# Hybrid RWKV-7 layer on one core: the jobs beside the triangular inverse in three pieces, the bonus sums later, the woven products spread to the inverse's middle

## The chip, the cores and the metric

One core of one Trainium2 chip runs the whole layer. The metric is the device time of one execution in microseconds (us), as the median of several runs.

## What is computed

One layer of a backbone that joins a bidirectional RWKV-7 recurrence and a neighbourhood attention, for 128 context tokens and 512 latent tokens of width 1024, all in float32. The change touches the recurrence alone. For every head (8 of them, 64 channels each) and each of two directions it is

```python
def _wkv_step(s, inp):
    r, w, k, v, a, b = inp
    sa = jnp.einsum("bhvk,bhk->bhv", s, a)
    s = s * w[:, :, None, :] + sa[..., None] * b[:, :, None, :] + v[..., None] * k[:, :, None, :]
    return s, jnp.einsum("bhvk,bhk->bhv", s, r)
...
    k_bonus = _heads(0.5 * (k_dir[:, :, 0] + k_dir[:, :, 1]))
    bonus = jnp.sum(rh * k_bonus * r_k, axis=-1, keepdims=True) * vh
    out = (y.astype(u.dtype) + bonus).reshape(bsz, t_len, RW_WIDTH) * gate
```

The kernel doesn't step through the tokens one by one. It cuts them into 10 chunks of 64 and solves each chunk with the inverse of a triangular matrix.

## The kernel before

**Groups and lines.** The 512 channels of the recurrence are four groups, ct = 0 to 3, of 128 channels (two heads). In a group there are 20 lines: 10 chunks in each direction. The groups run one after the other, and each has these stages, written as generators:

- `main`: the products that fill the triangular matrices Nt (`n_job`).
- `inv`: the inverse of all the 32x32 triangular blocks at once, on DVE, in 30 steps s (the multiplications L1315, L1322, L1329 and additions L1333), then two transposes (RT at L1346, T at L1348), products with the inverse on PE (L1359 and L1373), a copy on ACT (Hs, L1364) and copies on DVE and ACT into Rt (L1367, L1378).
- `carry`: the chunks in their order. Its first use of Rt is the matmul at L1449.
- `out`: the output of the group (L1498 to L1509), which runs beside the next group's inverse.

**Jobs.** The inverse is work of DVE. Beside it PE does jobs, at the steps s that the table `jobs` names. In groups 0 to 2 these are steps 2, 9 and 28, in group 3 steps 2, 8 and 28: a job of four lines first, then two jobs of eight lines. A job is `t_job` (L1274: transposes of B and K as 64x64 matmuls, 64 of them for eight lines, copied by ACT into TG) and then `g_job`, which has for each line two matmuls of the values (`turn`, L1252, or `flip`, L1263), two of L1216 (into the buffer pg) and four of L1219 (into the buffers pr): 128 matmuls for eight lines. `g_job` returns a function `masks`, which DVE runs at a later step (table `mds`; L1233 for pg and L1236 for pr). All of pg, pr, the t_job's buffers, and those of the bonus and of `out` are PSUM tiles of one tag, "w", with six buffers (`wps`).

**Bonus.** `bonus` is a generator too: one DVE operation (L1156), then for each half of the columns a matmul with a matrix of ones (L1162) and a DVE operation that multiplies it with v (L1164, in the trace by its tile bv).

**Woven products.** Between all of this PE does big products of other parts of the layer (L223 and L587; 128x128 weights, 320 columns), which depend on nothing of the group. `weave` sets the order: after each `yield` of a stage it takes one element "a.b.c" of the table `plan`, issues a products from the stream `fill`, b steps of the previous group's `out` and c steps of `bonus`.

```python
                p = next(plan)
                for _ in range(p[0]):
                    if not next(fill, False):
                        break
...
                weave(inv(ct, S, late), (og, bg))
```

The stream `fill` also carries the steps that are put off until so many products later. One of them is the shift of the next group's r and k (`shift`: L551 on ACT, L552 and L554 on DVE, tiles rt_ and kt_, first 128 columns, then 512). PE, DVE, ACT and POOL run these stages in the order in which the program is written (`manual_schedule`), so the plan decides what stands behind what on each engine.

Of the kernel before, what the change touches and what calls it, by code (L numbers as in the profile page):

```python
# [17 lines left out]
H2 = 320  # L18
# [13 lines left out]
        ("0.0.0 2.0.0 2.0.1 10.0.0 2.0.1 2.0.1 2.0.1 2.0.1 2.0.1 2.0.0 10.0.0 2.0.0 2.0.0 10.0.0 2.0.0 "  # L32
         "2.0.0 2.0.0 10.0.0 2.0.0 2.0.0 2.0.0 2.0.0 2.0.0 2.0.0 2.0.0 2.0.0 2.0.0 2.0.0 2.0.0 2.0.0 "
         "5.0.0 24.0.0 20.0.0 10.0.0 8.0.0 8.0.0 0.0.0"),
# [3 lines left out]
        ("0.0.0 0.0.0 2.0.1 10.0.0 1.0.0 2.1.1 2.1.1 2.1.1 2.1.1 1.1.1 10.0.0 3.1.0 2.0.0 2.0.0 2.0.0 "  # L38
         "2.1.0 2.1.0 10.0.0 2.1.0 2.1.0 2.1.0 2.1.0 2.1.0 2.1.0 12.0.0 2.0.0 2.0.0 2.0.0 2.0.0 2.0.0 "
         "5.0.0 24.0.0 20.0.0 10.0.0 8.0.0 8.0.0 0.0.0"),  # L40
# [3 lines left out]
        ("0.0.0 10.0.0 2.0.1 10.0.0 2.0.0 2.1.1 2.1.1 2.1.2 2.1.1 2.1.0 10.0.0 2.0.0 2.0.0 2.0.0 2.1.0 "  # L44
         "2.1.0 2.1.0 10.0.0 2.1.0 2.1.0 2.1.0 3.1.0 4.1.0 2.1.0 2.0.0 2.0.0 2.0.0 4.0.0 2.0.0 2.0.0 "
         "5.0.0 24.0.0 18.0.0 8.0.0 9.0.0 8.0.0 0.0.0"),
# [3 lines left out]
        ("0.0.0 16.1.0 8.1.1 9.0.0 2.1.0 8.1.1 1.1.1 0.1.1 0.1.1 0.1.1 4.1.0 14.1.0 6.1.0 6.1.0 6.1.0 "  # L50
         "6.1.0 6.1.0 7.1.0 6.0.0 6.0.0 6.0.0 6.0.0 6.0.0 6.0.0 7.0.0 6.0.0 6.0.0 6.0.0 6.0.0 6.0.0 "
         "6.0.0 6.0.0 11.0.0 8.0.0 8.0.0 2.0.0 0.0.0"),
# [25 lines left out]
    h2=0.91, jobs=((2, 9, 28), (2, 9, 28), (2, 9, 28), (2, 8, 28)),  # L78
    mds=((4, 12), (4, 12), (4, 12), (4, 12)), bud=((1.8, 0.8), (1.3, 1.8)), off=6, tk=2, h3=1,
# [35 lines left out]
def body(ctx: ExitStack, tc: tile.TileContext, xs, xp, cols, consts, w_ada, b_row, w_rw, w_qkv,  # L115
# [986 lines left out]
    with ExitStack() as s3:  # L1102
# [52 lines left out]
        def bonus(ct, S):  # L1155
            dve.scalar_tensor_tensor(out=S.bv, in0=S.bv, scalar=dcol(dhrk, ct), in1=rt_,  # L1156
                                     op0=ALU.mult, op1=ALU.mult)
            yield
            for hf in range(2):
                hs_ = slice(hf * H2, (hf + 1) * H2)  # L1160
                ps = wps()
                pe.matmul(ps[:, :H2], kc("blk1", 128), S.bv[:, hs_], start=True, stop=True)  # L1162
                yield
                dve.tensor_tensor(out=S.bv[:, hs_], in0=ps[:, :H2], in1=v[:, hs_], op=ALU.mult)  # L1164
                yield
            marks.add(f"R{ct}")
# [35 lines left out]
        def g_job(S, l0, l1):  # L1202
# [5 lines left out]
            for l in range(l0, l1):  # L1208
                if l0 == 0:
                    turn(pv, l, 0)  # L1210
                if l0 > 8:
                    flip(pv, l, f0)
                o_ = slice(64 * (l - l0), 64 * (l - l0) + 64)
                b, k = (S.BK[l // 10][:, l % 10, i, :] for i in range(2))
                for h in range(2):
                    pe.matmul(pg[hrows[1 - h], o_], k[hrows[h], :], AG[hrows[h], l, h, :], start=True, stop=True)  # L1216
                for x, i in ((b, 0), (k, 1)):
                    for h in range(2):
                        pe.matmul(pr[h][hrows[h ^ i], o_], x[hrows[h], :], R_[hrows[h], l, :],  # L1219
                                  start=True, stop=True)  # L1220
# [18 lines left out]
            return masks  # L1239
# [54 lines left out]
        def inv(ct, S, late):  # L1294
# [10 lines left out]
            masks = []  # L1305
            for s in range(1, 31):
# [870 lines left out]
```

## Time and profile before

| | |
|---|---|
| runs of the kernel, device us | 1145.75, 1146.5, 1142.03; median 1145.75 |
| the profiled execution's own time | 1141.53 us |
| its span in the profile | 1139.8 us, granted clock 0.997 |
| PE busy (matmuls) | 1106.1 us, 97% |
| DVE busy | 781.1 us, 69% |
| ACT busy | 533.7 us, 47% |
| POOL busy | 193.7 us, 17% |
| four groups of the recurrence, about 240 to 600 us of the span | PE busy 345.4 of 360 us |

How to read it: PE is TensorE, DVE VectorE, ACT ScalarE, POOL GpSimd. The span is the profiled execution from its first to its last record; the metric's time of that execution is 1.73 us longer. Busy shares are averages over the span. The rows below come from lists of waits and from timelines, whose times count from the span's start.

### The profile page before, as it was taken

To read this page: it belongs to the slowest core of one execution; us is meant where nothing else is said; L and a number is where in the kernel's file an instruction comes from. 1 tells how busy PE (TensorE), PEld (TensorE's weight loads), DVE (VectorE), ACT (ScalarE), POOL (GpSimd) and SP (SyncE) were. 2 spreads that over 40 slices of the span, in tenths; PEclk is the share of its full clock that TensorE was granted. 3 is DMA by queue.
4 is the path that set the end of the run, shared out by engine and by line. 5 is a ranking of instruction groups with operands and counts; after the bars stand their busy time and mean duration, and the time that the engine had idled before them with its cause. 6 is when DMAs were issued, how large, how long until landed. Compare 5 with 4: busy or idle time off the path is not lost.

```text
span 1139.8 us, 26864 instructions
## 1 busy us (share of the span) xinstructions
PE 1106.1 (97%) x11160; PEld 979.3 (86%) x11160; DVE 781.1 (69%) x1646; ACT 533.7 (47%) x1056; POOL 193.7 (17%) x261
## 2 busy tenths in 40 slices
PE   6999999999999999999899999999999999999998
PEld 4688878799888988888898788999899989998997
DVE  4565465769658948946777846996478647864776
ACT  4444566664574565566353525654134413441340
POOL 1163244320101211111100511200001010101000
PEclk9999999999999999999999999999999999999999
DMA  9752677654423443343734961223112321232122
GB/s 342 266 107 97 191 263 264 200 152 111 126 65 96 115 121 94 107 110 98 276 97 134 260 215 64 90 77 120 65 59 90 114 72 56 93 108 77 56 94 93
DMA packets 60482, 149.16 MB, mean 131 GB/s; under 512 B 7460, under 2 KB 22436, under 8 KB 60360
## 3 DMA queue, kind: packets, MB, share of 16 engines
q1 hardware_dynamic: 54312, 129.85, 35.0%
q0 software_dynamic: 4032, 14.68, 6.6%
q10 hardware_dynamic: 2016, 2.90, 0.8%
q8 instruction: 88, 1.44, 0.5%
q14 instruction: 34, 0.28, 0.1%
HBM read 118.41 MB, written 14.32 MB: 116 GB/s over the span
## 4 chain that ended last, share of the span: by engine, by line
PE 71%; DVE 11%; issue 7%; ACT 5%; DMA 5%; POOL 1%; SPq 0%; ACTq 0%; DVEq 0%; POOLq 0%
PE acc L311 23%; PE f L1880 21%; PE fl L223 9%; PE mm L223 4%; DMA wa<-in_w_ada_dram 2%; DVE RL L1333 1%; DVE pr L1329 1%; PE po L1011 1%; PE psa L1049 1%; PE pt L993 1%; PE lg L964 1%; DMA win<-in_rpbp_dram 1%; PE w L1449 1%; PE fl L587 1%; PE w L1462 1%
## 5 line engine op out<-in xcount | busy, mean ns | idle before, releaser
L1880 PE MATMUL f<-t,whi 128*128 128x320 f32 x640 | 141.7, 309 | 0.2
L311 PE MATMUL acc<-whi,u 128*128 128x512 f32 (+1 forms) x448 | 136.0, 385 | 0.0
L1880 PE MATMUL f<-b,whi 128*128 128x320 f32 x608 | 135.0, 310 | 0.4 <-DVE b L212 0.4
L223 PE MATMUL fl<-h,whi 128*128 128x320 f32 x672 | 121.6, 321 | 0.0
L1880 PEld LDWEIGHTS f<-t,whi 128*128 128x128 f32 x640 | 106.8, 188 | 0.8 <-issue 0.4
L223 PEld LDWEIGHTS fl<-h,whi 128*128 128x128 f32 x672 | 101.5, 188 | 4.9
L192 ACT CAST whi<-wst 128x1024 fp32r<-128x1024 f32 (+1 forms) x77 | 79.3, 1033 | 54.6 <-PE acc L311 28.3
L1880 PEld LDWEIGHTS f<-b,whi 128*128 128x128 f32 x608 | 101.7, 188 | 1.1 <-issue 0.6
L1880 PE MATMUL f<-t,wlo 128*128 128x320 f32 x320 | 98.9, 309 | 0.0
L311 PEld LDWEIGHTS acc<-whi,u 128*128 128x128 f32 x448 | 83.5, 188 | 16.6
L1880 PE MATMUL f<-b,wlo 128*128 128x320 f32 x304 | 94.0, 309 | 0.0
L1933 ACT CAST whi<-ws 128x1024 fp32r<-128x1024 f32 x40 | 42.0, 1051 | 104.5 <-PE f L1880 45.6
L311 PE MATMUL acc<-wlo,u 128*128 128x512 f32 (+1 forms) x224 | 86.3, 385 | 0.0
L1947 POOL TENSOR_TENSOR ws<-wst 128x512 f32<-128x512 f32 x20 | 28.9, 1447 | 334.9 <-DVE wlo L1936 226.3
L195 DVE TENSOR_TENSOR wlo<-wst,whi 128x1024 fp32r<-128x1024 f32 (+2 forms) x57 | 60.2, 1066 | 28.2 <-ACT whi L192 27.7
L311 PE MATMUL acc<-whi,h 128*128 128x512 f32 x240 | 78.5, 401 | 0.7 <-DVE h L436 0.7
L1748 DVE SCALAR_TENSOR_TENSOR tt<-acc,G 128x512 f32<-128x512 f32 (+1 forms) x51 | 34.7, 680 | 59.9 <-PE acc L311 44.6
L223 PE MATMUL fl<-h,wlo 128*128 128x320 f32 x336 | 63.3, 320 | 0.0
L1933 ACT CAST whi<-wst 128x1024 fp32r<-128x1024 f32 (+1 forms) x48 | 41.4, 870 | 42.3 <-PE acc L311 37.6
L191 POOL DMA_DIRECT2D wlo<-wst x28 | 24.8, 886 | 210.8 <-ACT wlo L190 194.9
L1880 PEld LDWEIGHTS f<-t,wlo 128*128 128x128 f32 x320 | 60.1, 188 | 0.0
L1936 DVE TENSOR_TENSOR wlo<-ws,whi 128x1024 fp32r<-128x1024 f32 x40 | 55.4, 1385 | 5.4 <-ACT whi L1933 5.4
(341 smaller groups left out, 2528.5 us busy)
## 6 DMA issues: line engine op xcount, KB each, us to landing
wst<-in_w_dram SPq DMA_DIRECT2D x66, 512.0 KB
wst<-in_w_rw_dram SPq DMA_DIRECT2D x31, 512.0 KB
wlo<-wst POOLq DMA_DIRECT2D x28, 512.0 KB, 4.8
wa<-in_w_ada_dram SPq DMA_DIRECT2D x24, 512.0 KB
f<-in_w_ada_dram SPq DMA_DIRECT2D x16, 512.0 KB
wst<-in_w_qkv_dram SPq DMA_DIRECT2D x12, 512.0 KB
o<-o_d SPq DMA_DIRECT2D x14, 320.0 KB
x<-in_xs_dram SPq DMA_DIRECT2D x8, 512.0 KB
```

The lines of the kernel that those rows point to most:

```text
L191: pool.dma_start(lo[:, :n].bitcast(F32), st[:, :n], accum_op=ALU.add)
L192: act.copy(hi[:, :n], st[:, :n])
L195: dve.tensor_tensor(out=lo[:, a:b], in0=st[:, a:b], in1=hi[:, a:b].bitcast(F32), op=ALU.subtract)
L223: pe.matmul(ps[:, :t1 - t0], w[:, a:a + 128], x[:, k0 + kt, t0:t1], start=n == 0, stop=n == 3 * nk - 1)
L311: pe.matmul(pss[i][:, a:b], lhs(x, kt, ts_), w[:, cs_], start=ki == 0 and n == 0, stop=ki == last and n == 2)
L587: pe.matmul(ps[hf][:, :H2], u[:, kt * 128:kt * 128 + 128], x[:, kt, a:b], start=kt == 0 and n == 0, stop=kt == 7 and n == 2)
L964: pe.matmul(psl[:, hd, o_:o_ + n], qT[ft][rows, qs], x[rows, :], start=True, stop=True)
L1748: dve.scalar_tensor_tensor(out=tt, in0=ps[:, a:b], scalar=c, in1=G[:, g, sl], op0=ALU.mult, op1=ALU.mult)
L1880: pe.matmul(ps[:, :H2], w_[:, c_], x_[:, kt, :], start=first and kt + n == 0, stop=last and kt == 3 and n == 2, skip_group_check=more)
L1933: act.copy(r[0][:, :width], src())
L1936: dve.tensor_tensor(out=r[1][:, :width], in0=src(), in1=r[0][:, :width].bitcast(F32), op=ALU.subtract)
L1947: eng_x(PRM["se"][i - 1]).tensor_tensor(out=o_, in0=x, in1=y, op=op)
```

## The change

1. `g_job` becomes a generator with one `yield` in its middle. For the jobs after step 5, `inv` runs `t_job` at step s, the first four lines of `g_job` at step s + 1 and the last four at step s + 2, so that a plan element, with its products, stands in each of the two gaps. The four-line job at step 2 is run at once as before.
2. The third job starts at step 26, not 28; in group 3 the second at step 9, not 8. The second masks are run at step 14, not 12.
3. In `bonus` both matmuls stand together, and the two DVE operations come later, one plan element apart.
4. The table `plan`: the number of products of each inverse is the same, but elements at the inverse's end give some to its middle. For group 2's inverse:

```diff
-        ("0.0.0 10.0.0 2.0.1 10.0.0 2.0.0 2.1.1 2.1.1 2.1.2 2.1.1 2.1.0 10.0.0 2.0.0 2.0.0 2.0.0 2.1.0 "
-         "2.1.0 2.1.0 10.0.0 2.1.0 2.1.0 2.1.0 3.1.0 4.1.0 2.1.0 2.0.0 2.0.0 2.0.0 4.0.0 2.0.0 2.0.0 "
-         "5.0.0 24.0.0 18.0.0 8.0.0 9.0.0 8.0.0 0.0.0"),
+        ("0.0.0 10.0.0 2.0.1 10.0.0 2.0.1 2.1.0 2.1.0 2.1.1 2.1.1 2.1.0 4.0.0 5.0.0 6.0.0 3.0.0 3.1.0 3.1.0 3.1.0 "
+         "6.0.0 3.1.0 3.1.0 3.1.0 3.1.0 3.1.0 3.1.0 3.0.0 3.0.0 3.0.0 4.0.0 4.0.0 4.0.0 4.0.0 16.0.0 16.0.0 8.0.0 "
+         "9.0.0 8.0.0 0.0.0"),
...
-    h2=0.91, jobs=((2, 9, 28), (2, 9, 28), (2, 9, 28), (2, 8, 28)),
-    mds=((4, 12), (4, 12), (4, 12), (4, 12)), bud=((1.8, 0.8), (1.3, 1.8)), off=6, tk=2, h3=1,
+    h2=0.91, jobs=((2, 9, 26),) * 4, mds=((4, 14),) * 4, bud=((1.8, 0.8), (1.3, 1.8)), off=6, tk=2, h3=1,
...
         def bonus(ct, S):
...
-            for hf in range(2):
-                hs_ = slice(hf * H2, (hf + 1) * H2)
-                ps = wps()
-                pe.matmul(ps[:, :H2], kc("blk1", 128), S.bv[:, hs_], start=True, stop=True)
-                yield
-                dve.tensor_tensor(out=S.bv[:, hs_], in0=ps[:, :H2], in1=v[:, hs_], op=ALU.mult)
-                yield
+            hs_ = [slice(hf * H2, (hf + 1) * H2) for hf in range(2)]
+            ps = [wps() for _ in hs_]
+            for p_, h_ in zip(ps, hs_):
+                pe.matmul(p_[:, :H2], kc("blk1", 128), S.bv[:, h_], start=True, stop=True)
+            yield
+            for n, (p_, h_) in enumerate(zip(ps, hs_)):
+                if n:
+                    yield
+                dve.tensor_tensor(out=S.bv[:, h_], in0=p_[:, :H2], in1=v[:, h_], op=ALU.mult)
...
-        def g_job(S, l0, l1):
+        def g_job(S, l0, l1, todo):
...
             for l in range(l0, l1):
+                if l == l0 + 4:
+                    yield 0
...
-            return masks
+            todo.append(masks)
...
-            masks = []
+            masks, begun = [], []
...
+                if begun and next(begun[0], None) is None:
+                    begun.pop()
                 if s in jobs:
                     for f in (v_job, t_job):
                         f(S, *jobs[s])
-                    masks.append(g_job(S, *jobs[s]))
+                    g = g_job(S, *jobs[s], masks)
+                    if s < 5:
+                        drain(g)
+                    else:
+                        begun.append(g)
                 yield
```

Lines of the changed kernel are some numbers off: L1274 is now L1277, L1216 is L1219, L1219 is L1222, L1252 is L1255, L1162 and L1164 are L1161 and L1166, L1346 is L1355, L552 is L551, L223 is L222, and L1502 is L1511.

**Three places in the order.** The first is PE in group 2's second job. Before, the g job's matmuls (first the values vp, then AG and R) follow the t job's (K into w_6206 and w_6207) at once:

```order
L1274 MATMUL w_6206<-K,f_833_5751 64x64
L1274 MATMUL w_6207<-K,f_833_5751 64x64
L1252 MATMUL w_6242<-K,vp_627 64x64 x2
L1216 MATMUL w_6243<-AG,f_833_5751 64x64 x2
L1219 MATMUL w_6244<-R__2901,f_833_5751 64x64
L1219 MATMUL w_6245<-R__2901,f_833_5751 64x64
```

In the change the end of the t job and the first g piece, and then the end of the first g piece and the second:

```order
L1277 MATMUL w_6207<-K,f_833_5751 64x64
L222 MATMUL fl_6139<-h_95,whi_5869 128x320
L222 MATMUL fl_6139<-h_92,whi_5869 128x320
L222 MATMUL fl_6139<-h_96,whi_5869 128x320
L222 MATMUL fl_6139<-h_92,whi_5869 128x320
L1255 MATMUL w_6250<-K,vp_627 64x64 x2
L1219 MATMUL w_6251<-AG,f_833_5751 64x64 x2
```

```order
L1222 MATMUL w_6253<-R__2901,f_833_5751 64x64
L222 MATMUL fl_6139<-h_96,whi_5869 128x320
L222 MATMUL fl_6139<-h_89,wlo_5870 128x320 x2
L222 MATMUL fl_6139<-h_90,wlo_5870 128x320 x2
L1255 MATMUL w_6250<-K,vp_627 64x64 x2
```

Four products of the stream now stand in the first gap and five in the second.

The second is DVE at the end of group 0's inverse, from the last step (L1322, now L1325) through the two transposes and the masks to the copies into Rt. Before:

```order
L1322 SCALAR_TENSOR_TENSOR RL_3044<-RL_3044 128x30
L1346 STREAM_TRANSPOSE f_602_3613<-RL_3044 128x1024
L1348 STREAM_TRANSPOSE f_603_3615<-RL_3044 128x1024
L1233 TENSOR_TENSOR AG<-w_3504,K 64x8x64 x2
L1236 TENSOR_TENSOR TG<-w_3505,K 128x8x64
L1236 TENSOR_TENSOR TG<-w_3506,K 128x8x64
L552 SCALAR_TENSOR_TENSOR rt__625<-U_3394,C,rt__625 128x128
L554 SCALAR_TENSOR_TENSOR rt__625<-U_3394,C,rt__625 128x128
L1367 COPY Rt<-f_603_3615 32x10x32 x8
```

In the change:

```order
L1325 SCALAR_TENSOR_TENSOR RL_3044<-RL_3044 128x30
L551 SCALAR_TENSOR_TENSOR rt__625<-U_3405,C,rt__625 128x128
L553 SCALAR_TENSOR_TENSOR rt__625<-U_3405,C,rt__625 128x128
L1355 STREAM_TRANSPOSE f_602_3621<-RL_3044 128x1024
L1357 STREAM_TRANSPOSE f_603_3623<-RL_3044 128x1024
L1236 TENSOR_TENSOR AG<-w_3503,K 64x8x64 x2
L1239 TENSOR_TENSOR TG<-w_3504,K 128x8x64
L1239 TENSOR_TENSOR TG<-w_3505,K 128x8x64
L1376 COPY Rt<-f_603_3623 32x10x32 x8
```

The shift of the next group's r, 128 columns, moved from behind the masks to ahead of the first transpose.

The third is DVE in group 3 at the inverse's fifth to eighth steps; RL and pr are the inverse's tiles, out_7446 is the output of group 2 and bv_7334 the bonus of group 3. Before:

```order
L1333 TENSOR_TENSOR RL_7568<-RL_7568,pr_7609 128x13x5 x2
L1164 TENSOR_TENSOR bv_7334<-w_7727,vp_627 128x320
L1329 TENSOR_TENSOR pr_7609<-RL_7568 128x72
L1329 TENSOR_TENSOR pr_7609<-RL_7568 128x78
L1333 TENSOR_TENSOR RL_7568<-RL_7568,pr_7609 128x12x6
L1333 TENSOR_TENSOR RL_7568<-RL_7568,pr_7609 128x13x6
L1498 TENSOR_TENSOR out_7446<-out_7446,w_7734 128x512
L1499 TENSOR_TENSOR out_7446<-out_7446,w_7735 128x128
L1329 TENSOR_TENSOR pr_7609<-RL_7568 128x84 x2
L1333 TENSOR_TENSOR RL_7568<-RL_7568,pr_7609 128x12x7 x2
L1502 TENSOR_TENSOR out_7446<-out_7446,bv_5768 128x640
L1164 TENSOR_TENSOR bv_7334<-w_7749,vp_627 128x320
```

In the change:

```order
L1336 TENSOR_TENSOR RL_7568<-RL_7568,pr_7609 128x13x6
L1507 TENSOR_TENSOR out_7446<-out_7446,w_7736 128x512
L1508 TENSOR_TENSOR out_7446<-out_7446,w_7737 128x128
L1332 TENSOR_TENSOR pr_7609<-RL_7568 128x84 x2
L1336 TENSOR_TENSOR RL_7568<-RL_7568,pr_7609 128x12x7 x2
L1511 TENSOR_TENSOR out_7446<-out_7446,bv_5768 128x640
L1166 TENSOR_TENSOR bv_7334<-w_7710,vp_627 128x320
L1332 TENSOR_TENSOR pr_7609<-RL_7568 128x88
L1332 TENSOR_TENSOR pr_7609<-RL_7568 128x96
L1336 TENSOR_TENSOR RL_7568<-RL_7568,pr_7609 128x11x8
L1336 TENSOR_TENSOR RL_7568<-RL_7568,pr_7609 128x12x8
L1166 TENSOR_TENSOR bv_7334<-w_7711,vp_627 128x320
```

The first bonus sum moved behind the output's last addition, and the second from there to one step later.

## Rows read from the trace of the kernel before

**Rows 1.** Page, busy time, DMA queues (packets, MB, share), chain by engine.

```profile
PE 1106.1 (97%) x11160; PEld 979.3 (86%) x11160; DVE 781.1 (69%) x1646; ACT 533.7 (47%) x1056; POOL 193.7 (17%) x261
...
q8 instruction: 88, 1.44, 0.5%
...
PE 71%; DVE 11%; issue 7%; ACT 5%; DMA 5%; POOL 1%; SPq 0%; ACTq 0%; DVEq 0%; POOLq 0%
```

**Rows 2.** Waits of PE: line, releaser, us in total, times, longest us.

```profile
PE w L1219 <- issue: 2.5, 2, 1.3
...
PE w L1216 <- issue: 1.4, 1, 1.4
...
PE w L1449 <- DVE Rt L1378: 0.9, 1, 0.9
```

**Rows 3.** Timeline of PE, group 0's third job: start, duration, line, count.

```profile
274.11 2.51 PE L223 MATMUL fl<-h,whi 128*128 128x320 f32 x16
276.45 0.75 PE L223 MATMUL fl<-h,wlo 128*128 128x320 f32 x4
277.13 1.16 PE L1274 MATMUL w<-K,f 64*64 64x64 f32 x64
...
280.09 0.86 PE L223 MATMUL fl<-h,wlo 128*128 128x320 f32 x4
280.78 2.50 PE L223 MATMUL fl<-h,whi 128*128 128x320 f32 x16
```

**Rows 4.** Timeline of PE, group 2's second job.

```profile
454.06 0.28 PE L1219 MATMUL w<-R__2901,f 64*64 64x64 f32 x4
455.56 0.27 PE L1219 MATMUL w<-R__2901,f 64*64 64x64 f32 x2 [1.21 <-issue]
```

**Rows 5.** Timeline of PE, group 2's third job.

```profile
469.35 0.22 PE L1216 MATMUL w<-AG,f 64*64 64x64 f32 x1
470.96 0.27 PE L1216 MATMUL w<-AG,f 64*64 64x64 f32 x1 [1.39 <-issue]
```

**Rows 6.** Timeline of PE, group 3's second job.

```profile
550.84 0.28 PE L1219 MATMUL w<-R__2901,f 64*64 64x64 f32 x2
552.74 0.28 PE L1219 MATMUL w<-R__2901,f 64*64 64x64 f32 x3 [1.63 <-DVE bv L1164]
...
553.91 0.22 PE L1216 MATMUL w<-AG,f 64*64 64x64 f32 x2
555.40 0.28 PE L1219 MATMUL w<-R__2901,f 64*64 64x64 f32 x4 [1.27 <-issue]
```

**Rows 7.** DMA queues between 453 and 455 us: packets, MB, share.

```profile
q8 instruction: 1, 0.02, 3.2%
```

**Rows 8.** Timeline of DVE, group 3's second bonus sum and the step behind it.

```profile
552.21 0.48 DVE L1164 TENSOR_TENSOR bv<-w,vp 128x320 f32<-128x320 f32 x1
552.61 0.41 DVE L1329 TENSOR_TENSOR pr<-RL 128x88 f32<-128x88 f32 x2
...
553.29 0.43 DVE L1329 TENSOR_TENSOR pr<-RL 128x99 f32<-128x99 f32 x2
```

**Rows 9.** Timeline of DVE, group 0: first bonus sum, first transpose.

```profile
262.98 0.49 DVE L1164 TENSOR_TENSOR bv<-w,vp 128x320 f32<-128x320 f32 x1 [0.18 <-PE w L1162]
...
285.51 2.06 DVE L1346 STREAM_TRANSPOSE f<-RL 128x1024 f32<-128x1024 f32 x1
```

**Rows 10.** Timeline of ACT, group 0's rt_ of 128 columns.

```profile
285.02 0.40 ACT L551 ACTIVATE rt__625<-U,D 128x128 f32<-128x128 f32 x1
```

**Rows 11.** Timeline of PE, group 1's first products with the inverse.

```profile
385.17 1.46 PE L1359 MATMUL w<-f,Nt 32*32 32x32 f32 x80 [0.35 <-DVE f L1346]
```

**Rows 12.** Timeline of DVE, group 2: second bonus sum, first transpose.

```profile
451.31 0.49 DVE L1164 TENSOR_TENSOR bv<-w,vp 128x320 f32<-128x320 f32 x1 [2.09 <-PE w L1162]
...
476.12 2.07 DVE L1346 STREAM_TRANSPOSE f<-RL 128x1024 f32<-128x1024 f32 x1
```

**Rows 13.** Timeline of PE, group 2's first products with the inverse.

```profile
479.12 1.48 PE L1359 MATMUL w<-f,Nt 32*32 32x32 f32 x80
```

More of the change, by code (lines that the diff above doesn't have):

```diff
@@ L31 @@
         "22.0 0.0 2.0 4.0",
-        ("0.0.0 2.0.0 2.0.1 10.0.0 2.0.1 2.0.1 2.0.1 2.0.1 2.0.1 2.0.0 10.0.0 2.0.0 2.0.0 10.0.0 2.0.0 "
-         "2.0.0 2.0.0 10.0.0 2.0.0 2.0.0 2.0.0 2.0.0 2.0.0 2.0.0 2.0.0 2.0.0 2.0.0 2.0.0 2.0.0 2.0.0 "
-         "5.0.0 24.0.0 20.0.0 10.0.0 8.0.0 8.0.0 0.0.0"),
+        ("0.0.0 2.0.0 2.0.1 10.0.0 2.0.1 2.0.0 2.0.0 2.0.0 2.0.1 2.0.1 4.0.0 5.0.0 6.0.0 4.0.0 3.0.0 3.0.0 3.0.0 "
+         "5.0.0 3.0.0 3.0.0 3.0.0 3.0.0 3.0.0 3.0.0 3.0.0 3.0.0 3.0.0 4.0.0 4.0.0 4.0.0 4.0.0 20.0.0 18.0.0 9.0.0 "
+         "8.0.0 8.0.0 0.0.0"),
         ("10.0 1.0 7.1 5.2 0.0 7.1 7.2 0.0 7.1 7.2 0.0 8.1 12.2 0.0 7.1 7.2 0.0 7.1 7.2 0.0 6.1 6.2 "
@@ L37 @@
         "8.0 2.0 9.0 9.0",
-        ("0.0.0 0.0.0 2.0.1 10.0.0 1.0.0 2.1.1 2.1.1 2.1.1 2.1.1 1.1.1 10.0.0 3.1.0 2.0.0 2.0.0 2.0.0 "
-         "2.1.0 2.1.0 10.0.0 2.1.0 2.1.0 2.1.0 2.1.0 2.1.0 2.1.0 12.0.0 2.0.0 2.0.0 2.0.0 2.0.0 2.0.0 "
-         "5.0.0 24.0.0 20.0.0 10.0.0 8.0.0 8.0.0 0.0.0"),
+        ("0.0.0 0.0.0 2.0.1 10.0.0 1.0.1 2.1.0 2.1.0 2.1.0 2.1.1 1.1.1 4.0.0 5.1.0 6.0.0 3.0.0 3.0.0 3.1.0 3.1.0 "
+         "6.0.0 3.1.0 3.1.0 3.1.0 3.1.0 3.1.0 3.1.0 8.0.0 3.0.0 3.0.0 4.0.0 4.0.0 4.0.0 4.0.0 18.0.0 18.0.0 9.0.0 "
+         "8.0.0 8.0.0 0.0.0"),
         ("10.0 0.0 7.1 7.2 0.0 7.1 7.2 0.0 7.1 7.2 0.0 7.1 7.2 0.0 7.1 7.2 0.0 6.1 7.2 0.0 7.1 7.2 0.0 "
@@ L49 @@
         "16.2 0.0 8.0 8.0",
-        ("0.0.0 16.1.0 8.1.1 9.0.0 2.1.0 8.1.1 1.1.1 0.1.1 0.1.1 0.1.1 4.1.0 14.1.0 6.1.0 6.1.0 6.1.0 "
-         "6.1.0 6.1.0 7.1.0 6.0.0 6.0.0 6.0.0 6.0.0 6.0.0 6.0.0 7.0.0 6.0.0 6.0.0 6.0.0 6.0.0 6.0.0 "
-         "6.0.0 6.0.0 11.0.0 8.0.0 8.0.0 2.0.0 0.0.0"),
+        ("0.0.0 16.1.0 8.1.1 9.0.0 2.1.1 8.1.0 1.1.0 1.1.0 1.1.1 1.1.1 4.1.0 6.1.0 6.1.0 6.1.0 6.1.0 6.1.0 6.1.0 "
+         "7.1.0 6.0.0 6.0.0 6.0.0 6.0.0 6.0.0 6.0.0 7.0.0 6.0.0 6.0.0 6.0.0 6.0.0 6.0.0 6.0.0 11.0.0 11.0.0 8.0.0 "
+         "8.0.0 2.0.0 0.0.0"),
         ("10.3 0.0 5.1 5.2 0.0 5.1 5.2 0.0 5.1 5.2 0.0 5.1 5.2 0.0 5.1 5.2 0.0 5.1 5.2 0.0 5.1 5.2 0.0 "
```

## Prediction, made before the changed kernel ran

> **What bounds the kernel now.** I read the page first: PE is busy for 97% of the span and the chain that ended last lies mostly on PE [rows 1]. So the change can gain only what PE stands idle inside the recurrence, and it can lose whatever new gaps or waits it puts on PE. The plan moves woven products, it removes none, and the same matmuls, sums and casts are issued as before, so no engine gets less work.
>
> Then I read the waits of PE, since that list names the idle time. The reader is to see that the largest ones of the inverse are on the job lines L1219 and L1216, that their releaser is "issue" (PE waited for nothing that the profile shows), and that only one other wait of PE that the change can reach is near a microsecond, L1449 on DVE's copy L1378 [rows 2].
>
> Then the timeline of PE over one eight-line job at a time. Group 0's third job is how an undisturbed job looks [rows 3]: 64 transposing matmuls at L1274 and 128 more of the g job run from 277.13 to 280.09, that is 2.96 us for 192 matmuls, 15.4 ns each. There are eight such jobs after step 5 (two in each of four groups), and three of them are torn. Group 2's second job stands still after 454.06 until 455.56 [rows 4]; with some 0.06 us for the four matmuls of the first row that is 1.44 us. Its third job stands still from 469.35 to 470.96, less one matmul 1.59 us [rows 5]. Group 3's second job loses time twice: 552.74 - 550.84 = 1.90, less two matmuls 1.87 us, behind DVE's bonus sum L1164, and 1.46 us (553.91 to 555.40, less two matmuls) behind "issue" [rows 6].
>
> What is "issue"? During group 2's stall one packet of the queue named "instruction" moved, of 0.02 MB [rows 7], and over the span that queue moved 88 packets with 1.44 MB, 16 KB each [rows 1]. PE alone issues 22,320 matmuls and weight loads [rows 1], and 1.44 MB over these is 64 bytes. So a packet holds some 256 of them, which a burst of 128 matmuls with their loads uses up in 1.97 us at the rate above. My reading: in a burst PE uses its instructions up faster than the next packet comes, and where a packet is late it stands still for 1.2 to 1.4 us.
>
> **The change part by part.** All sums are against the profiled execution of 1141.53 us, which is 1.73 us above its span; it lies 4.22 us under the median of the three runs, 1145.75 us.
>
> *(a) Jobs in three pieces.* Each job after step 5 is now 64 matmuls, four or five products, 64 matmuls, five or six products, 64 matmuls. A product costs (276.45 - 274.11)/16 = 0.146 us [rows 3]. Nine of them are 1.31 us in which PE takes few instructions, about as long as the stalls. If the packets are asked for in step with the instructions used, the late packet comes while products run, and the three issue stalls go: 1.44 + 1.59 + 1.46 = 4.49 us. Bounds: 0 (the packet boundary lies elsewhere, and the stalls with it) and -4.5. I take -4.5, because five of the eight bursts already run without a stall, so little help is needed, and because the gap takes the place of the stall at nearly its size. The products were run at the inverse's end before, so they cost nothing new.
>
> By the Trainium skill (page "Runtime: NRT & Kernel Launch", section "Instruction fetch mechanics") instructions come in blocks of 16 KiB, 256 of them, and the fetch of the next is hidden behind the one that runs. The size of the packets here agrees with it; the waits with "issue" behind them, 2.5 and 1.4 us in all, do not look hidden. If the rule held strictly, these stalls would have another cause and term (a) would be 0, which is rival B's sum.
>
> *(b) More changes between products and small matmuls.* Around an undisturbed job, four products before it take 277.13 - 276.45 = 0.68 us and four after it 0.69 us, where 4 x 0.146 is 0.585 [rows 3]: about 0.1 us for each change from one kind to the other. Each job gets two more gaps, so four more changes, 0.38 us. In groups 2 and 3 that is four jobs x 0.38 = +1.5 us on PE, and nothing covers it there. Bounds 0 (the stretches overlap the modelled ends of the matmuls) and +1.5; I take +1.5, since the same 0.1 stands on both sides of the burst. Groups 0 and 1 are under (d).
>
> *(c) Bonus sums later, group 3.* Both L1162 matmuls now stand together and take two PSUM buffers out of six, until DVE's sums free them; the g pieces behind them use the same tag. In group 3 the first sum now stands behind the output's addition L1502 and so begins where the second one did, at 552.21; the second comes one step of the inverse later. The sum holds DVE until 552.61, the step's four operations until 553.29 [rows 8], so the second sum ends near 552.21 + 0.40 + 0.68 + 0.48 = 553.77. PE reaches the buffer later too: three merge products and one product of the output, of 320 columns as well (4 x 0.146 = 0.58), and the four gap products with two changes of 0.1 (0.78) now stand ahead of it, 550.84 + 1.36 = 552.2. So PE waits for about 1.57 us where it waited for 1.87: -0.3. Bounds: -1.9 (the wait goes) and +0.5 (PE arrives as early as before and waits for the later sum). I take the worked value. What is queued behind the waiting matmul are the rest of the g pieces and all products of PE after them, so the wait counts in full.
>
> *(d) The end of the inverse, groups 0 and 1.* In group 0 DVE runs from its first bonus wait, 0.18 us, to L1378 without another gap, and PE waits 0.87 us for that copy at L1449 [rows 2, 9]. So here DVE's chain sets the end and hides PE's 0.76 us of new changes. But the change puts the two rt_ shifts of 128 columns, which stood behind the transposes and masks, ahead of the first transpose. They need ACT's rt_ at L551, which ends at 285.02 + 0.40 = 285.42 [rows 10]; ACT's copies wait for the last product of that stage, which PE reaches 0.76 us later, so 286.2. DVE arrives at 285.51 - 0.18 = 285.33 [rows 9], and stands still for 0.85 us. Net for L1378 and so for L1449: +0.85 - 0.18 = +0.7 us; bounds -0.2 (no delay of ACT and the old wait gone) and +1.5 (PE's own delay adds to the wait). In group 1 PE waits for the first transpose already, 0.35 us [rows 11]: 0.76 for the changes plus 0.15 for the one product that moves ahead of L1359, less that wait and less the product that is then missing behind, is +0.4, bounds 0 and +0.9.
>
> In group 2 PE gains 1.44 + 1.59 - 0.76 = 2.27 us ahead of L1359, and the first transpose is ahead of it by 479.12 - 476.12 - 2.07 = 0.93 us now [rows 12, 13]. DVE gains there too, since its waits for the bonus products go (2.09 us at the second [rows 12]; the matmul now stands earlier on PE). So I cost L1359's wait at nothing; if DVE gained nothing it would be 2.27 - 0.93 = 1.3 us.
>
> Sum: -4.5 + 1.5 - 0.3 + 0.7 + 0.4 = -2.2 us. The profiled execution would be 1139.3, and the median 1145.75 - 2.2 = **1143.6 us**. Best ends: -4.5 - 1.9 - 0.2 = -6.6, 1139.2. Worst ends, group 2's L1359 with them: 1.5 + 0.5 + 1.5 + 0.9 + 1.3 = +5.7, 1151.5.
>
> **Rivals.** *B, the stalls stay.* A burst is still 64 matmuls without a product, and five jobs had no stall without any gap, so where a packet ends may matter more than how dense the burst is; moving instructions can also put an end into a job that had none. Then (a) is 0: -2.2 + 4.5 = +2.3, 1148.0. Against it: a gap of 0.6 to 0.9 us stands beside every piece.
>
> *C, nothing is given back.* The 0.1 us at each change is only how matmul ends are modelled, group 0 finds ACT early, and the bonus wait goes: the best ends, 1139.2. For it: PE's idle time at L1449 covers group 0. Against it: DVE's row order in group 3, where the second sum is a step later than before.
>
> *D, the other side: the later sums hold PSUM, and PE waits for DVE in every group.* Place: the first or second g piece of each second job, whose buffers are those of the two bonus products. Price: group 3's wait, 1.87 us [rows 6], in all four groups, 7.5 us in place of 1.87: 1143.6 + 0.3 + 5.6 = 1149.5; with the stalls staying too, 1154.0. It decides where PE comes to a piece before DVE's second sum is done. For it: group 3 does it now. Against it: in groups 0 to 2 nothing of an output's additions stands ahead of the sums, and the four gap products give DVE 0.78 us more.
>
> **How the numbers follow.** Forecast 0.57, B 0.17, C 0.17, D 0.09. A measurement of this kernel can tell about 0.5%, 5.7 us, from no change. The forecast, B and most of D lie within it; C lies at its edge (1139.2 against 1140.0), and with a little of the forecast's tail gives 0.16 for faster; D with the stalls gives 0.06 for slower; 0.78 is left for the same. The range 1138.0 to 1149.0 takes in B, the forecast's bounds and C with about a microsecond for the runs' own spread; it leaves out D's worse half and the worst ends.
>
> **What would show it.** (a) right: no row of the eight jobs with "issue" as releaser; wrong: a stall over 1 us in any piece. (b) right: about 0.1 us at each change; wrong: none, or over 0.2. (c) right: one wait of 1.2 to 1.9 us on the bonus sum in group 3's second job; wrong: none, or others in groups 0 to 2 (D). (d) right: DVE idle before group 0's rt_ shift for about 0.9 us behind ACT, and PE's wait at L1449 still there. A forecast over 5 us off would mean that these terms are not where the time went, above all if PE's products or the stages after the recurrence took another length than before.

## The result and the profile after

The changed kernel took 1146.73 us (median of 20 runs), the kernel before 1142.88 us in the same comparison. The ratio on record is 1.0023, 95% interval 1.0015 to 1.0031, so it is slower by 2.6 us (1.7 to 3.5); the two medians alone lie 3.85 us apart. The forecast was 1143.6, faster by 2.2, counted from 1145.75, the median of the three runs known then. The time lies inside the range given and within half a per cent, but on the other side of no change.

The profiled execution of the change took 1143.92 us, with a span of 1142.1; it is the second shortest of the 20. The waits of its PE (line, releaser, us in total, times, longest us):

```profile
PE fl L222 <- ACT fl L594: 2.1, 1, 2.1
...
PE w L1146 <- ACT pre L1141: 1.7, 1, 1.7
PE w L1195 <- issue: 1.1, 1, 1.1
...
PE w L1368 <- DVE f L1355: 0.4, 1, 0.4
```

The "issue" waits of the jobs [rows 2] are gone, and so is the wait at the first use of Rt. In their place stand two waits on ACT that the kernel before did not have at this size, at the merge products in group 3 and at the output's transposes in group 2.

Where the time went is read from the timelines: for each group the time from its first matmul of L1194 (L1195 in the change) to the next group's, for the last group to the start of its last L1449 matmuls. The rows below the first two are the experiments, each under its name; "timed" is the ratio to the kernel before on the same chip.

| kernel | group 0 | group 1 | group 2 | group 3 | sum | timed, 95% interval |
|---|---|---|---|---|---|---|
| before | 90.63 | 92.58 | 98.38 | 84.04 | 365.63 | |
| changed | 91.60 | 93.44 | 98.40 | 84.39 | 367.83 | 1.0023 (1.0015 to 1.0031) |
| e1_whole | 90.44 | 92.83 | 99.93 | 85.56 | 368.76 | 1.0033 (1.0022 to 1.0044) |
| e2_pieces | 90.43 | 93.86 | 98.04 | 83.20 | 365.53 | 0.9988 (0.9977 to 0.9999) |
| e3_sums | 91.70 | 92.97 | 97.84 | 84.20 | 366.71 | 1.0012 (1.0001 to 1.0023) |
| e4_align | 90.10 | 92.64 | 96.79 | 84.30 | 363.83 | 0.9987 (0.9978 to 0.9995) |
| x12_align40 | 90.90 | 92.62 | 97.66 | 83.21 | 364.39 | 0.9978 (0.9969 to 0.9987) |
| e5_plan | 91.41 | 92.47 | 99.43 | 85.87 | 369.18 | 1.0022 (1.0008 to 1.0037) |
| e8_oldsums | 92.53 | 93.44 | 98.24 | 86.34 | 370.55 | 1.0021 (1.0005 to 1.0038) |
| e6_ct2 | 90.96 | 93.42 | 96.85 | 85.84 | 367.07 | 0.9999 (0.9985 to 1.0013) |
| x13_ct0 | 90.31 | 93.42 | 98.37 | 85.88 | 367.98 | 1.0001 (0.9987 to 1.0014) |
| x10_ct23 | 91.28 | 93.44 | 96.82 | 82.98 | 364.52 | 0.9993 (0.9982 to 1.0003) |
| e7_three | 91.02 | 92.58 | 98.11 | 83.18 | 364.89 | 0.9970 (0.9958 to 0.9983) |
| x9_best | 91.18 | 92.60 | 96.81 | 83.08 | 363.67 | 0.9957 (0.9944 to 0.9970) |

The change lost 0.97 us in group 0, 0.86 in group 1, nothing in group 2 and 0.35 in group 3, 2.2 in all, about as much as its span is longer (2.3). Group 2 is the surprise: the forecast had -2.27 us there.

Group 0 holds two things that differ between executions of the same instructions. One is the first wait of PE on issue, at L1194, in the kernel before:

```profile
PE w L1194 <- issue: 0.6, 1, 0.6
```

It is 0.57 us there, 0.58 in e4_align and 0.85 in x12_align40, whose instructions up to this place are the same, and 1.13 in the change. The other is a short fall of the granted clock near 300 us (last section), which the profile of the kernel before has and that of the change has not. e4_align has the instructions of the kernel before in group 0, and no fall. Against it, with the first waits taken off, the change lost 91.60 - 1.13 - (90.10 - 0.58) = 0.95 us. So the two cancel here, and differences of half a microsecond in this column mean nothing by themselves.

**One gap.** The timeline of PE in the change, group 0's third job (start, duration, line, count):

```profile
278.18 1.16 PE L1277 MATMUL w<-K,f 64*64 64x64 f32 x64
279.27 0.86 PE L222 MATMUL fl<-h,wlo 128*128 128x320 f32 x4
280.06 0.27 PE L1266 MATMUL w<-ZV,J 64*64 64x64 f32 x2
...
283.02 1.14 PE L222 MATMUL fl<-h,whi 128*128 128x320 f32 x6
```

From 278.18 to 283.02 are 4.84 us. Eight products of 0.146 are 1.17, so the job itself takes 3.67 where it took 2.96 [rows 3]: 0.71 us for two gaps, 0.35 for each. Of the 0.71, 0.10 lies in each of the three pieces (1.09 us for 64 matmuls, where a third of 2.96 is 0.99) and 0.20 in each of the two runs of products (0.79 for four).

**Group 2.** The timeline of ACT in the change, and that of the kernel before at the same place:

```profile
460.04 0.44 ACT L572 ACTIVATE fl<-fl 128x320 f32<-128x320 f32 x1
460.37 1.05 ACT L189 ACTIVATE wlo<-wst 128x1024 fp32r<-128x1024 f32 x1
461.32 1.03 ACT L191 CAST whi<-wst 128x1024 fp32r<-128x1024 f32 x1
462.25 0.72 ACT L1141 COPY pre<-r 128x640 f32<-128x640 f32 x1
```

```profile
458.54 0.44 ACT L573 ACTIVATE fl<-fl 128x320 f32<-128x320 f32 x1 [1.16 <-issue]
458.87 0.72 ACT L1142 COPY pre<-r 128x640 f32<-128x640 f32 x1
459.49 1.06 ACT L190 ACTIVATE wlo<-wst 128x1024 fp32r<-128x1024 f32 x1
```

The two casts of the next weights are put off until so many products later. The plan issues more products ahead of the output's step, so the casts, 1.05 and 1.03 us, now stand ahead of the copy that this step needs, and ACT works in the order in which its steps are issued. PE, at the output's transposes L1146:

```profile
463.03 0.77 PE L1146 MATMUL w<-K,pre 128*128 128x128 f32 x5 [1.72 <-ACT pre L1141]
```

**Group 3.** ACT and then PE of the change:

```profile
552.61 0.92 ACT L1509 ACTIVATE out<-out,C 128x640 f32<-128x640 f32 x1 [4.33 <-DVE out L1508]
553.43 0.74 ACT L594 ACTIVATE fl<-fl 128x320 f32<-128x320 f32 x2
```

```profile
553.90 0.71 PE L222 MATMUL fl<-o,whi 128*128 128x320 f32 x3 [2.14 <-ACT fl L594]
```

The kernel before, ACT and then PE: the products of the same kind (from o into fl) come only behind the job, 4.5 us after ACT's L595 has ended.

```profile
551.34 0.74 ACT L595 ACTIVATE fl<-fl 128x320 f32<-128x320 f32 x2
```

```profile
556.54 1.57 PE L223 MATMUL fl<-o,whi 128*128 128x320 f32 x8
```

The three merge products that the plan, with the job's later step, brought ahead of the job write an fl tile that ACT's L594 has to empty first, and L594 stands behind the output's L1509, which waits for DVE. So PE waits 2.14 us there, and the wait for the bonus sum [rows 6] is gone because PE comes late to it.

**Group 0.** DVE and PE of the change at the end of the inverse:

```profile
287.58 0.35 DVE L551 SCALAR_TENSOR_TENSOR rt__625<-U,C,rt__625 128x128 f32<-128x128 f32 x1 [1.05 <-ACT rt__625 L550]
```

```profile
290.48 1.48 PE L1368 MATMUL w<-f,Nt 32*32 32x32 f32 x80 [0.44 <-DVE f L1355]
```

DVE waits 1.05 us for ACT's rt_ before the first transpose, and PE 0.44 us for the transpose.

### The profile page after: what moved, and what is told of

The parts are those of the page before. It is cut to its first block, busy times and chain, and to the rows that moved or that the text cites. A ratio compares the mean times of both kernels' runs of the same rounds, so it can differ in the third digit from the quotient of the medians.

```text
span 1142.1 us, 26860 instructions
## 1 busy us (share of the span) xinstructions
PE 1108.1 (97%) x11160; PEld 977.8 (86%) x11160; DVE 781.9 (68%) x1646; ACT 534.4 (47%) x1056; POOL 194.6 (17%) x261
## 4 chain that ended last, share of the span: by engine, by line
PE 77%; DVE 7%; issue 7%; DMA 5%; ACT 4%; POOL 0%; SPq 0%; ACTq 0%; DVEq 0%; POOLq 0%
PE acc L310 23%; PE f L1889 21%; PE fl L222 12%; PE mm L222 5%; DMA wa<-in_w_ada_dram 2%; PE lg L963 1%; PE po L1010 1%; PE pt L992 1%; PE psa L1048 1%; DMA win<-in_rpbp_dram 1%; DMA f<-in_w_ada_dram 1%; PE w L1458 1%; PE w L1277 1%; PE w L1222 1%; DMA o<-o_d 1%
## 5 line engine op out<-in xcount | busy, mean ns | idle before, releaser
L222 PE MATMUL fl<-h,whi 128*128 128x320 f32 x672 | 123.9, 321 | 0.0
L222 PEld LDWEIGHTS fl<-h,whi 128*128 128x128 f32 x672 | 101.2, 188 | 5.4
L222 PE MATMUL fl<-h,wlo 128*128 128x320 f32 x336 | 62.9, 318 | 0.0
```

Source lines behind the costliest of these rows:

```text
L222: pe.matmul(ps[:, :t1 - t0], w[:, a:a + 128], x[:, k0 + kt, t0:t1], start=n == 0, stop=n == 3 * nk - 1)
```

## The experiments

Two theories stood at first: G, that gaps cost and stalls go, with the rest in what the plan moves along; and P, that the plan and the later sums make the loss and the pieces do nothing. In the diffs, the unchanged end of a long line is left out.

**e1_whole.** The change with its jobs whole:

```diff
-                    if s < 5:
+                    if True:
                         drain(g)
```

> The changed kernel with every job whole again (plan, later sums and job steps stay). Theory G (gaps): each of the 16 gaps costs 0.33 us on PE (0.13 leaving the small matmuls, 0.11 inside the first products, 0.09 going back), so 5.3 us go; the three issue stalls of 1.4 to 1.6 us in groups 2 and 3 come back, 4.6 us, and the one in group 2's second job hides the new wait for ACT at L1146 (1.7 us) again. So 0.7 to 2.3 us less than the changed kernel, about 0 to +1.7 us against the kernel before. Rival P (plan and sums alone): the pieces cost and save nothing, so the time is that of the changed kernel, +2.4 us against before.

Measured: +3.8 us against before, about 1.1 more than the change (0.9 by the sums of the table; the timed intervals overlap). That is outside both theories' numbers, but on the side on which the pieces help. Of the three stalls the two of group 2 came back, at the same places as before; PE's timeline:

```profile
455.85 0.28 PE L1222 MATMUL w<-R__2901,f 64*64 64x64 f32 x2 [0.84 <-issue]
...
472.58 0.21 PE L1219 MATMUL w<-AG,f 64*64 64x64 f32 x1 [1.26 <-issue]
```

The stall of group 3 did not come back: its second job, whole here as in the kernel before, has no wait on issue. The wait for ACT's copy L1141 was still 1.47 us, so the stall hid 0.25 us of it, and that part of G was wrong.

**e2_pieces.** The kernel before with pieces alone (the diff of `g_job` and `inv` as in the change; the plan of group 2 as an example):

```diff
-2.1.0 10.0.0 2.0.0 2.0.0
+2.1.0 4.0.0 5.0.0 5.0.0
...
-2.0.0 5.0.0 24.0.0
+4.0.0 4.0.0 23.0.0
```

> The kernel before with its eight jobs in three pieces and nothing else; the products in the gaps are taken from the two elements beside them. Theory G: +5.3 us for 16 gaps, -4.6 us for three stalls that go, so +0.7 us against before, with no wait over 0.3 us on issue in a job. Rival S (the stalls only move): they stay, and it is +5.3 us. Rival P: within 0.3 us of before.

Measured: -1.4 us (-2.6 to -0.1), better than all three expectations. Group 1, which had no stall to lose, shows the price of four gaps: 93.86 - 92.58 = 1.28 us. Group 0 shows no price: with the first wait taken off it takes 90.43 - 0.97 = 89.46 us, and e4_align's 89.52. Group 3 gains 0.84. Group 2 gains 0.34 only, where the stalls (1.53 + 1.65 us by the length of its jobs) less four gaps would give 1.8. At the inverse's first product 0.9 of it is there: the third job in pieces takes 0.4 us more than the others, and PE waits 0.41 us for ACT's copy at the output's transposes, where it waited 0.16. Another 0.55 goes between the inverse's first product and the first use of Rt, with a new wait on issue among the products with the inverse:

```profile
487.22 0.40 PE L1369 MATMUL w<-f,Hs 32*32 32x32 f32 x12 [0.34 <-issue]
```

**e3_sums.** The kernel before with the later sums alone:

```diff
-2.0.1 2.0.1 2.0.1 2.0.1 2.0.1 2.0.0
+2.0.1 2.0.0 2.0.0 2.0.0 2.0.1 2.0.1
```

(elements 4 to 9 of group 0; `bonus` as in the change.)

> The kernel before with both bonus matmuls together and the two sums later, and nothing else. Theory G: PE waits longer for group 3's second sum, 2.5 to 3 us in place of 1.87, and nowhere else, so +0.6 to +1.1 us. Rival P: the later sums are what costs, +2 us or more, with waits in other groups too.

Measured: +1.4 us (+0.1 to +2.6), in line with G in size, not in place: group 3's job waits 1.74 us, for ACT's copy of the t job's buffer, where it waited 1.63 for the sum. That the sums hold two of the six PSUM buffers at once is the likely reason, which no run takes apart. Another group has a new wait, as P had it: group 0's second job takes 3.75 us in place of 2.96.

**e4_align and x12_align40.** The kernel before, with the values' transposing matmuls of one job of group 1 repeated, so that all later instructions of PE move by 64 or by 40 (the diff is e4_align's):

```diff
+            extra.append(0)
+            for _ in range(5 if len(extra) == 2 else 1):
+                for l in range(8, 10):
+                    turn(pv, l, 8)
```

> The kernel before with 16 transposing matmuls of group 1's values issued four times over (32 records of 15 ns, 0.5 us; they write the same values again), so that every PE instruction behind them lies 64 instructions later in its 16 KB packet. Theory F (an issue stall comes where a job begins some 55 instructions ahead of a packet's end, so that a second end falls into its burst): the three stalls in groups 2 and 3 go without any gap, -4.6 + 0.5 = -4.1 us against before; a smaller new one can come at the very end of group 3's third job. Rival D (a dense burst stalls by itself, wherever the packets end): the stalls stay, +0.5 us.

> The kernel before with five more repetitions of one line's transposing matmuls in group 1 (20 records, 0.3 us), so that all later PE instructions lie 40 later in their 16 KB packet. With the packets' ends where the stalls were, an end now falls within the first 20 instructions of the torn jobs or just one into each job. Theory F: no wait on issue over 0.4 us in any of the eight jobs, neither the three of the kernel before nor the one that 64 instructions brought to group 3's third job; in group 2's third job about 1 us is handed to a wait for the output's addition that the stall hid. -4.6 + 0.3 + 1.1 = about -3 us against before. Rival: stalls come back at other places of the jobs, and it is as with 64 instructions, -1.5.

Measured: -1.5 and -2.5 us. With 64, the three issue stalls are gone without any gap, and one came where it was expected, near the end of group 3's third job, at the 188th of 192 matmuls:

```profile
577.91 0.34 PE L1219 MATMUL w<-R__2901,f 64*64 64x64 f32 x5 [1.54 <-issue]
```

With 40, no job has a wait on issue over 0.36 us:

```profile
455.58 0.34 PE L1219 MATMUL w<-R__2901,f 64*64 64x64 f32 x8 [0.36 <-issue]
```

So a stall belongs to the place of a packet's end in the job, theory F, and not to a dense burst as such. The place can be worked out from the traces. In the kernel before, e1_whole, e3_sums and e5_plan PE stood still behind 150 to 156 matmuls of the job, in e4_align behind 187, and in x12_align40, for the 0.36 us, behind 136. Each matmul has its load, and a packet holds 256 instructions, so if this is a job's second packet end, the first lies 44 to 56, 118 and 16 instructions behind the job's start. Counted on from there through the records of PE, the whole jobs without a stall have their first end at 22 or less, or only one end. There is one exception: in e1_whole and e5_plan group 3's second job has its first end at 40 and no stall. Whether the place or the wait of 2.1 to 2.5 us just ahead of that job spares it is open.

What F did not give is the full size. With 64, the time won was handed on, in group 2's third job to 0.91 us for DVE's addition of the output, and to the new stall. With 40, two new waits on issue stand outside the jobs, 0.46 us behind group 3's third job and 0.59 us among group 2's products with the inverse:

```profile
484.42 0.64 PE L1377 MATMUL w<-f,Hs 32*32 32x32 f32 x32 [0.59 <-issue]
```

**e5_plan.** The kernel before with the numbers alone:

```diff
-    h2=0.91, jobs=((2, 9, 28), (2, 9, 28), (2, 9, 28), (2, 8, 28)),
-    mds=((4, 12), (4, 12), (4, 12), (4, 12)),
+    h2=0.91, jobs=((2, 9, 26),) * 4, mds=((4, 14),) * 4,
```

(and the first two numbers of each plan element of the change.)

> The kernel before with the new numbers alone: products moved to the middle, the jobs' and masks' new steps; jobs whole, bonus sums as before. Theory A (what the plan moves with the products costs: in group 2 two weight casts of ACT, 2.1 us, now stand ahead of the output's copy that PE waits for, in group 3 three merge products wait for ACT, in group 0 the rt_ shift holds back the first transpose): +1.5 to +4 us against before, with a wait of 1 to 2 us at the output's transposes in group 2, less what a stall in the job ahead hides, and one near 2 us on the fl tile in group 3. Rival I (the loss needs pieces and sums together): within 0.7 us of before.

Measured: +2.5 us, theory A. The waits in groups 2 and 3 are those of the change, in PE's timeline:

```profile
462.42 0.77 PE L1134 MATMUL w<-K,pre 128*128 128x128 f32 x5 [1.47 <-ACT pre L1129]
...
554.24 0.42 PE L210 MATMUL fl<-o,whi 128*128 128x320 f32 x1 [2.54 <-ACT fl L582]
```

The moved numbers alone cost about as much as the whole change (0.9 to 4.2 against 1.7 to 3.5 us). With whole jobs the two stalls of group 2 are there, 0.74 and 0.98 us, and none in group 3.

**e6_ct2.** The change with one step of the output in group 2 two elements earlier:

```diff
-6.0.0 3.0.0 3.1.0
+6.1.0 3.0.0 3.0.0
```

> The changed kernel with one step of the output in group 2's inverse two elements earlier, so that ACT does the copy L1141 ahead of the casts L189 and L191, as in the kernel before. Theory A: the 1.7 us wait at L1146 falls under 0.3, so -1.4 to -1.6 us against the changed kernel, about +1 us against before. Rival: PE then waits as long somewhere else in group 2 (for RT at L1368 by up to 1.3 us), and nothing is won.

Measured: the time of the kernel before (-1.7 to +1.5 us), so about 2.6 us better than the change. ACT's queue again, and PE behind it:

```profile
460.05 0.72 ACT L1129 COPY pre<-r 128x640 f32<-128x640 f32 x1
460.80 0.44 ACT L560 ACTIVATE fl<-fl 128x320 f32<-128x320 f32 x1
461.13 1.05 ACT L177 ACTIVATE wlo<-wst 128x1024 fp32r<-128x1024 f32 x1
```

```profile
461.29 0.71 PE L1134 MATMUL w<-K,pre 128*128 128x128 f32 x5
```

The copy stands ahead of the casts, PE no longer waits, and the group is 1.55 us shorter, nearly the whole of the wait (1.72). So but for this, group 2 would have gained 1.53 us of the 2.27 forecast.

**e8_oldsums.** The change with the bonus as before.

```diff
-            ps = [wps() for _ in hs_]
+            for hf in range(2):
...
+                dve.tensor_tensor(out=S.bv[:, hs_], in0=ps[:, :H2], in1=v[:, hs_], op=ALU.mult)
+                yield
```

> The changed kernel with the bonus as before (each matmul followed by its sum, at the old elements). Theory A: the three merge products in group 3 still wait for ACT's L594 for about 2 us and hide the sums, so little goes: 0 to -1 us against the changed kernel, +1.5 to +2.5 against before. Rival P (the later sums are a cause of their own): -1.4 us against the changed kernel or more, as the sums alone cost 1.4 us on the kernel before.

Measured: +2.4 us against before (0.6 to 4.3), as the change and as theory A had it; the interval takes in P's number too, 1.2. The traces speak for A: no job waits for a sum, here or in the change, and the wait on the fl tile (here 2.54 us) stands ahead of the sums in group 3.

**x13_ct0 and x10_ct23.** The change with group 0, or with groups 2 and 3, mended (plan elements, sums and job steps of the kernel before in groups 0 or 3, e6_ct2's in group 2; pieces stay):

```diff
-    h2=0.91, jobs=((2, 9, 26),) * 4, mds=((4, 14),) * 4,
+    h2=0.91, jobs=((2, 9, 28),) + ((2, 9, 26),) * 3, mds=((4, 12),) + ((4, 14),) * 3,
...
-    h2=0.91, jobs=((2, 9, 26),) * 4, mds=((4, 14),) * 4,
+    h2=0.91, jobs=((2, 9, 26),) * 3 + ((2, 8, 28),), mds=((4, 14),) * 3 + ((4, 12),),
```

> The changed kernel with group 0 alone as in the kernel before (products, sums, job steps; its jobs stay in pieces). Theory: the rt_ shift ahead of group 0's first transpose costs 0.7 to 0.9 us there: DVE no longer waits for ACT's rt_, PE waits again at the first use of Rt, and the group falls from 91.6 to about 90.4 us in the profile (0.5 of it was a longer wait on issue at the start that is not of the change). The other groups stay, so about +1.7 us against before. Rival: the shift costs nothing since PE's gaps are then the bound, and the group stays above 91 us.

> The changed kernel with two places mended: the output's step in group 2 two elements earlier, and group 3 with its old products, sums and job steps (pieces stay in all eight jobs). Theory A: the 2.1 us wait on the fl tile in group 3 goes, PE waits about 1 us for the bonus sum there, -1.2 us against the version with group 2 mended alone and -1.2 to -1.6 us against before; fewer executions have the clock's fall in group 3 that this version showed at 554 us. Rival: the wait at the fl tile cost nothing (it only hid the wait for the sums), and the time is that of before.

Measured: the first +0.1 us against before (-1.5 to +1.6), 2.5 better than the change; its group 0 fell from 91.60 to 90.31, of which 0.3 is a shorter wait on issue at L1195. It takes back the products, sums and steps of group 0 together, so the 1.0 us left is not the shift's alone. DVE goes into the transposes without a wait:

```profile
286.05 2.09 DVE L1352 STREAM_TRANSPOSE f<-RL 128x1024 f32<-128x1024 f32 x1
291.81 0.34 DVE L539 SCALAR_TENSOR_TENSOR rt__625<-U,C,rt__625 128x128 f32<-128x128 f32 x1
```

PE did not wait again at the first use of Rt: its own gaps made it late, so that detail was a miss. The second took -0.8 us (-2.1 to +0.3), and its group 3 82.98 us where the change has 84.39, 1.41 less; the 2.14 us on the fl tile became 0.91, and none is left for the sum.

**e7_three and x9_best.** The kernel before with pieces in the three torn jobs alone; and the parts that paid: groups 0 and 1 as before, group 2 of e6_ct2, group 3 of e7_three. The first hunk, in both, is against the change; the second, of x9_best alone, against the kernel before:

```diff
-                    if s < 5:
+                    if s < 5 or ct < 2 or ct == 3 and s > 20:
                         drain(g)
...
-    h2=0.91, jobs=((2, 9, 28), (2, 9, 28), (2, 9, 28), (2, 8, 28)),
-    mds=((4, 12), (4, 12), (4, 12), (4, 12)),
+    h2=0.91, jobs=((2, 9, 28), (2, 9, 28), (2, 9, 26), (2, 8, 28)),
+    mds=((4, 12), (4, 12), (4, 14), (4, 12)),
```

> The kernel before with pieces in three jobs alone: both jobs of eight lines in group 2 and the first of them in group 3; products from the elements beside the gaps. Theory G: the three issue stalls go (4.6 us), 0.8 us of the bonus wait in group 3 too, and six gaps cost 2.0 us: -3 us against before, 1.3 to 2 us less than with pieces in all eight jobs. Rival: stalls on issue turn up in jobs that are whole, and it is no better than with eight.

> A version from the parts that paid: groups 0 and 1 as in the kernel before; group 2 as in the changed kernel with the output's step two elements earlier; group 3 as in the kernel before with its first eight-line job in pieces. Theory A + G: the profiles of these groups were 90.1 to 91.0, 92.6, 96.85 and 83.2 us (from one group's first matmul to the next's) against 90.6, 92.6, 98.4 and 84.0 before, so -2 to -3 us in the profile, and -3 to -5 us timed, as the three pieces alone gave -3.4. Rival: the parts don't add, since group 2 then only hands its wait to group 3 (DVE's chain or ACT's L583), and it is no better than -3.4.

Measured: -3.4 us (-4.8 to -1.9) and -4.9 us (-6.4 to -3.4); the second was 1139.55 us (median of five runs) where the kernel before took 1144.34, and beats both kernels of this case. A wait on issue of 0.65 and of 0.52 us is left in the last piece of group 3's job in these two. In group 2 of x9_best the transposes do not wait, in PE's timeline:

```profile
458.26 1.77 PE L211 MATMUL fl<-h,whi 128*128 128x320 f32 x11
459.87 0.71 PE L1135 MATMUL w<-K,pre 128*128 128x128 f32 x5
```

## Why the prediction was wrong

- **(a) the three issue stalls go, -4.5:** right in what came of it: no piece of the change waits on issue. The reason was right in part. In group 2 the pieces did it, since with whole jobs both waits are back (e1_whole, e5_plan). In group 3 that is not shown, since there the stall stayed away with whole jobs too. And what counts is where the packets end (e4_align, x12_align40), as rival B argued; pieces do not always help fully (0.65 and 0.52 us are left in e7_three and x9_best). The rule of the Trainium skill (page "Runtime: NRT & Kernel Launch", section "Instruction fetch mechanics"), that the fetch is mostly hidden, does not hold in the torn bursts: 0.74 to 1.54 us were not. Its blocks of 256 instructions fit.
- **(b) the gaps, 0.38 us a job:** mis-sized. A job in three pieces costs 0.71 us, not 0.38. I divided the whole job by its matmuls (15.4 ns) and so put the cost of leaving it into their rate; a piece of 64 takes 1.09 us, not 0.99. In groups 2 and 3 that is 1.3 us more than the forecast's 1.5, in group 1 0.7 us more; in group 0 the gaps hide behind DVE, as forecast (e2_pieces).
- **"The products were run at the inverse's end before, so they cost nothing new":** the step that failed. The plan's numbers do not only place products. Every step of ACT and DVE that is put off until so many products later moves with them: the casts ahead of L1141 (1.55 us in group 2, taken back by e6_ct2, which moves one step alone), and the merge products come to stand ahead of L594 (a wait of 2.14 us in group 3; 1.41 us come back where x10_ct23 has the old numbers and sums). e5_plan shows that these numbers alone cost about what the change costs. I had compared the order of PE and DVE at the places that I priced, and left out ACT's.
- **(c) group 3's sum:** the forecast wait of 1.57 us is not there. The sums come as forecast (the second ends at 555.39 + 0.48 = 555.87; forecast 553.77, and the group starts 1.96 us later), but PE waits 2.14 us earlier on, for the fl tile, and so comes late to them. Net of stall, sum, gaps and this wait: -3.44 for the second job (6.40 to 2.96) + 1.42 + 2.14, and 0.25 for two more changes at the output's products, is +0.37; measured +0.35, forecast -1.0.
- **(d) groups 0 and 1:** the mechanism was right (DVE behind ACT's rt_ for 1.05 us, forecast 0.85), the sum 1.8 us in place of 1.1: group 0 lost 0.97 (0.95 against e4_align) and group 1 0.86, its gaps being dearer. The wait at L1449, a sign that the forecast named, is not there: PE's own gaps and its wait for the transpose make it late.
- **Group 2:** -3.18 for the stalls by the jobs' lengths, +1.42 for four gaps, +1.55 and +0.16 for ACT's copies is -0.05; measured +0.02, forecast -2.27.
- **The rivals:** B gave nearly the right change, +2.3 us, by a mechanism that did not occur. D did not occur: no job of the change waits for a sum. The loss came from a mechanism that no rival had.
- **Luck:** that the time lies in the range is no merit of the sum. The forecast started 2.9 us above the median of the 20 runs, and that hid part of its error in the change itself (-2.2 us forecast, +2.6 measured).

## What to carry to other kernels

Where a table places filler work, ask of every engine what else rides on it: steps that are put off by a count of fillers move with them, and on an engine that works in order a 1 us cast that slips ahead of a 0.7 us copy is paid by whoever waits for the copy. A gap between two kinds of matmuls has a price (0.35 us here), so open one only where it removes a wait: group 1, with no stall, lost 1.28 us to four gaps. Three of eight jobs in pieces came out at -3.4 us and eight at -1.4, though these intervals overlap. A stall on issue in a long burst of short instructions depends on where the burst begins in the instruction stream; moving the bursts by 40 instructions took it out of the jobs, and brought smaller ones elsewhere.

## What the runs showed of the hardware that I had not expected

The granted clock fell to its lower level, 1.2 of 2.4 GHz, in short stretches after PE had stood idle. In the profile of the kernel before it did so behind the 0.87 us wait in group 0: the mean clock (third column from the end) is 0.67 in this stretch, 0.50 in the next two microseconds and 0.96 in the one behind them:

```profile
299.00:301.00 2.00, 1.96 (x16) 1.89 (x17) 0.00 (x0) 1.31 (x5) 0.00 (x0) 0.67 0.96 369
```

Seven of the fourteen profiles have such a fall in group 0, behind waits of 0.67 to 0.88 us; e4_align has the wait of 0.88 and no fall. From the first use of Rt to the next group's first matmul the kernel before took 45.86 us and e4_align, with the same instructions, 45.35, so the fall cost 0.5 us there.

Of the six profiled kernels with the wait of 2.1 to 2.5 us on the fl tile in group 3, three (e6_ct2, e8_oldsums, x13_ct0) show such a fall right behind it, of the eight without that wait none. The stretch from 553 to 557 us of e6_ct2 and of the change (the same columns; PE's busy time stands first behind the length):

```profile
553.00:557.00 4.00, 4.00 (x84) 3.11 (x86) 2.13 (x10) 1.64 (x3) 0.00 (x0) 0.64 0.47 172
```

```profile
553.00:557.00 4.00, 3.10 (x77) 2.40 (x77) 3.20 (x13) 1.89 (x5) 0.00 (x0) 1.00 0.76 288
```

Group 3 of e6_ct2 is 1.45 us longer (85.84 against 84.39), with the same instructions there. So a wait can cost more than its length, in some executions. The timed gains of x13_ct0 and e6_ct2 over the change (2.5 and 2.6 us) are larger than those of their groups in the profiles (1.3 and 1.55). The falls do not explain that, since both versions keep the wait on the fl tile and both profiles have the fall behind it; the intervals are wide enough to leave it open.
